# A long-convolution and recurrence block on one core: spectra and DFT tables kept as two parts in memory

## Chip, cores and metric

One Trainium2 chip, one of its cores. The metric is the time of one execution in device microseconds. The times shown are of three runs of the kernel before, and of one profiled execution of it.

## What is computed

A block over 4096 tokens of width 1024: RMSNorm, one input projection to 4608 columns, two mixers side by side, a gated norm of each, one output projection, the residual and a last norm. What matters here is the first mixer, a long convolution of 768 channels over the whole sequence, done through Fourier transforms of length 8192:

```python
def _fft_conv(u, k):
    L = u.shape[1]
    U = jnp.fft.rfft(u, n=2 * L, axis=1)
    K = jnp.fft.rfft(k, n=2 * L, axis=0)
    return jnp.fft.irfft(U * K[None], n=2 * L, axis=1)[:, :L]

        u = v * x1
        y_hy = x0 * (_fft_conv(u, kfilt) + hy_skip[l].astype(f32) * u)
```

`kfilt` comes from a small network over positions (the filter). The second mixer is a gated linear recurrence (RG-LRU) of 768 channels in both directions.

## The kernel before

Every float32 operand of a matmul is split into two parts of a type that TensorE (PE) takes in one pass, `hi` = the value rounded and `lo` = the value less `hi`; three matmuls (hi hi, hi lo, lo hi) then give the product (`mm3`, L503 to L507). A split is a ScalarE copy that rounds and a subtraction (`split`, L499 to L501).

The projection goes in steps: one step is one block of 128 of the 36 x 128 output columns for one of 8 chunks of 512 tokens, 24 matmuls (L311 to L313), 288 steps in all, in five passes over the chunks; the first pass makes the normalised input `x` in two parts and stores it (`xs`), later passes load it. The weights of a pass are loaded in halves of 256 KB (L277) and split on VectorE (L278, L279).

The transform of length 8192 is done as 128 x 64. Four stages belong to it:

- `phase_filter` (L509): a small network, and then 64 rounds, each of which makes one 128 x 768 slice of the filter, splits it into `kr`, multiplies it by the table `fa` (`first_dft`, L573 to L577), evicts the result into `kw` and stores it in `ef_d`.
- `phase_u` (L620): 32 groups of two slices of `u`; each is loaded, split into `ut` (L635, L636), multiplied by `fu`, evicted into `ustg` (L644) and stored in `eu_d` (L645).
- `phase_mid` (L653): 65 steps. Step k loads a 128 x 768 slice of `ef_d` and of `eu_d` and splits both (L658 to L660: a ScalarE copy and a GpSimd subtraction for each), loads the tables of this k (L665) and splits them on GpSimd (L669, L670), multiplies both slices by the first table, forms the complex product on VectorE (L689 to L692), splits it (`rs`, L500, L501), multiplies by the second table, evicts into `r` and stores in `ey_d` (L702, L703).
- `phase_iy` (L721): 32 groups that load two slices of `ey_d` (L736), split them into `es` (L738, L739), multiply by `fi` (L745) and store the result (L751).

`phase_lru` is the recurrence, `phase_out` (L754) the output projection; it begins when both mixers are done.

The generators are woven by `weave`: the program is written so that projection steps alternate with the steps of one other stage (filter, then recurrence, then u, mid and iy) by fixed weights. What the engines get is another order: `TileContext(..., schedule_with_timeline_sim=True)` reorders the instructions of all engines by an estimate of when each could run. The order is fixed before the run, and each engine works through its own in order; an instruction that waits holds up those behind it. All loads and stores but a few are issued by SP's queue, in one order; a load from SP waits for the eighth load or store before it to have landed.

The lines that the prediction speaks of:

## Time and profile before

| | us |
|---|---|
| median of 3 runs (lowest to highest) | 2957.67 (2956.57 to 2961.78) |
| the profiled execution, its own time | 2955.19 |
| span of the profile, first to last instruction | 2953.4 |
| PE busy | 2848.1 |
| VectorE (DVE) busy | 1997.9 |
| ScalarE (ACT) busy | 1697.9 |
| GpSimd (POOL) busy | 705.9 |

The stages by the trace: the first 8 projection steps run until about 61 us, the filter's network until about 200 us, the filter's rounds from 221 to 668 us, the recurrence from 678 to about 1400 us, u from 1402 to 1562 us, the middle stage from 1576 to 2176 us, the inverse stage from 2187 to 2343 us, the output from 2362 us on. Projection steps run beside all of them until 2329 us.

A row of a window gives the window, its length, the busy us and the number of instructions of each engine (PEld is PE's loading of weights), the share of its full clock that PE was granted, the mean busy share of the 16 DMA engines, and GB/s. "busy" of PE is not its rate: a matmul of 512 columns lasts 0.39 us, but the next starts 0.227 us after it.

### The profile page before, as it was taken

What the parts mean: (1) busy time and instruction counts of PE and PEld (TensorE: products, weight loads), DVE (VectorE), ACT (ScalarE), POOL (GpSimd) and SP (SyncE); (2) the same over time, 40 slices, a digit from 0 to 9 for tenths busy, and PEclk for the clock granted to TensorE, in tenths of its full rate; (3) what the DMA queues carried; (4) which work ended last, traced back from release to release, by engine and by line L of the source; (5) the groups of instructions that cost most, each with busy time, mean ns of one, the idle gap of its engine ahead of it and who ended that gap; (6) DMA issues with size and microseconds to landing.
All of it is one profiled execution on the core that took longest, in us unless ns stands there. A gap on an engine that the chain in (4) does not pass through costs nothing.

```text
span 2953.4 us, 37821 instructions
## 1 busy us (share of the span) xinstructions
PE 2848.1 (96%) x13211; PEld 2386.2 (81%) x13211; DVE 1997.9 (68%) x2144; ACT 1697.9 (57%) x2534; POOL 705.9 (24%) x910
## 2 busy tenths in 40 slices
PE   7999999999999999999999998999999799999998
PEld 6778888888887787877888887888888678888886
DVE  6998879664768856787664788666643366666665
ACT  4678887767787676764445675666645432222222
POOL 0013323210101201111004776766710010000001
PEclk9999999999999999999999999999999889999999
DMA  7566657437879877787997677666679865455542
GB/s 273 210 219 235 232 215 250 177 136 244 292 273 309 291 277 249 258 310 225 357 342 277 227 239 259 230 231 238 235 276 309 280 211 164 164 182 169 176 154 75
DMA packets 338238, 699.33 MB, mean 237 GB/s; under 512 B 33821, under 2 KB 156145, under 8 KB 337791
## 3 DMA queue, kind: packets, MB, share of 16 engines
q1 hardware_dynamic: 337918, 696.85, 67.9%
q8 instruction: 105, 1.72, 0.2%
q14 instruction: 87, 0.70, 0.1%
q0 software_dynamic: 128, 0.05, 0.0%
HBM read 445.13 MB, written 251.66 MB: 236 GB/s over the span
## 4 chain that ended last, share of the span: by engine, by line
PE 65%; DVE 13%; DMA 9%; issue 5%; ACT 5%; POOL 3%; SPq 1%; DVEq 0%; ACTq 0%; POOLq 0%
PE mm L311 12%; PE mm L312 12%; PE mm L313 12%; PE aux L506 8%; PE aux L819 4%; PE aux L817 4%; PE aux L818 4%; PE aux L443 3%; DVE cv L343 2%; PE aux L745 2%; DMA eu<-eud 2%; DMA x<-xs 2%; DVE sy L796 2%; PE aux L642 2%; DVE bb L470 1%
## 5 line engine op out<-in xcount | busy, mean ns | idle before, releaser
L311 PE MATMUL mm<-x,w 128*128 128x512 f32 x2304 | 909.3, 396 | 12.6 <-ACT cv L341 5.6
L312 PE MATMUL mm<-x,w 128*128 128x512 f32 x2304 | 907.6, 394 | 0.1
L313 PE MATMUL mm<-x,w 128*128 128x512 f32 x2304 | 905.2, 394 | 0.0
L311 PEld LDWEIGHTS mm<-x,w 128*128 128x128 f32 x2304 | 435.2, 189 | 105.3 <-DMA x<-xs 9.3
L313 PEld LDWEIGHTS mm<-x,w 128*128 128x128 f32 x2304 | 434.7, 189 | 84.4 <-issue 0.5
L312 PEld LDWEIGHTS mm<-x,w 128*128 128x128 f32 x2304 | 434.9, 189 | 84.1 <-issue 1.4
L817 PE MATMUL aux<-w,A 128*128 128x512 f32 x768 | 305.7, 398 | 19.0 <-DMA y<-yld 19.0
L343 DVE SCALAR_TENSOR_TENSOR cv<-raw,cols,cv 128x512 f32<-128x512 f32 (+2 forms) x336 | 260.7, 780 | 85.7 <-ACT cv L341 81.2
L819 PE MATMUL aux<-w,A 128*128 128x512 f32 x768 | 305.2, 401 | 0.0
L818 PE MATMUL aux<-w,A 128*128 128x512 f32 x768 | 304.4, 396 | 0.0
L798 POOL CAST sr<-sy 128x256 fp32r<-128x256 f32 x32 | 39.2, 1226 | 703.4 <-DVE sy L796 498.2
L660 POOL TENSOR_TENSOR ef<-ef 128x768 fp32r<-128x768 f32 x64 | 129.1, 2017 | 239.3 <-DMA eu<-eud 195.2
L817 PEld LDWEIGHTS aux<-w,A 128*128 128x128 f32 x768 | 146.1, 190 | 49.6 <-ACT A L793 19.3
L818 PEld LDWEIGHTS aux<-w,A 128*128 128x128 f32 x768 | 146.0, 190 | 32.0
L819 PEld LDWEIGHTS aux<-w,A 128*128 128x128 f32 x768 | 145.9, 190 | 30.9
L501 DVE TENSOR_TENSOR rs<-r,rs 128x768 fp32r<-128x768 f32 x65 | 94.1, 1447 | 108.3 <-ACT rs L500 108.3
L791 ACT ACTIVATE y<-y 128x1536 f32<-128x1536 f32 x32 | 47.7, 1490 | 202.8 <-DVE S L790 180.9
L333 ACT ACTIVATE raw<-mm 128x512 f32<-128x512 f32 x192 | 113.3, 590 | 86.0 <-PE mm L313 85.6
L443 PE MATMUL aux<-hl,wg 128*128 128x512 f32 x576 | 147.8, 392 | 5.4 <-ACT bb L445 5.2
L477 POOL TENSOR_TENSOR xb<-xb,bb 128x1024 f32<-128x1024 f32 x24 | 65.2, 2719 | 292.5 <-DVE bb L470 203.6
L660 POOL TENSOR_TENSOR eu<-eu 128x768 fp32r<-128x768 f32 x64 | 124.3, 1943 | 39.0 <-ACT eu L659 38.9
L443 PEld LDWEIGHTS aux<-hl,wg 128*128 128x128 f32 x576 | 107.3, 188 | 29.3 <-ACT bb L445 6.8
(201 smaller groups left out, 5023.6 us busy)
## 6 DMA issues: line engine op xcount, KB each, us to landing
x<-xs SPq DMA_DIRECT2D x256, 512.0 KB
hl<-hld SPq DMA_DIRECT2D x96, 512.0 KB
xs<-x SPq DMA_DIRECT2D x64, 512.0 KB
efd<-kw SPq DMA_DIRECT2D x64, 384.0 KB
sd<-cv SPq DMA_DIRECT2D x96, 256.0 KB
xb<-xbd SPq DMA_DIRECT2D x48, 512.0 KB
eud<-ustg SPq DMA_DIRECT2D x32, 768.0 KB
ef<-efd SPq DMA_DIRECT2D x64, 384.0 KB
```

The source lines that it names most:

```text
L311: nc.tensor.matmul(ps, lhsT=w[:, 0, kt, :], rhs=x[kt][:, 0], start=kt == 0, stop=False)
L312: nc.tensor.matmul(ps, lhsT=w[:, 0, kt, :], rhs=x[kt][:, 1], start=False, stop=False)
L313: nc.tensor.matmul(ps, lhsT=w[:, 1, kt, :], rhs=x[kt][:, 0], start=False, stop=kt == KT - 1)
L333: nc.scalar.activation(R[:, K - 1:K - 1 + TC], ps, AF.Copy)
L343: nc.vector.scalar_tensor_tensor(y[:, :N], R[:, k:k + N], w[k], y[:, :N], op0=ALU.mult, op1=ALU.add)
L443: nc.tensor.matmul(ps[:, h], lhsT=wg[:, u, gi, :], rhs=hl[h][:, v], start=k == 0, stop=k == 2)
L501: nc.vector.tensor_tensor(dst[:, 1], src, dst[:, 0].bitcast(F32), ALU.subtract)
L506: nc.tensor.matmul(ps[:, h, :NH], lhsT=lhs[:, x], rhs=rhs[:, y, h * NH:(h + 1) * NH], start=first and i == 0, stop=last and i == 2)
L660: eng.tensor_tensor(t[:, 1], raw, t[:, 0].bitcast(F32), ALU.subtract)
L817: nc.tensor.matmul(ps[:, h], lhsT=ht, rhs=w[:, 0, sl], start=b == 0, stop=False)
L818: nc.tensor.matmul(ps[:, h], lhsT=ht, rhs=w[:, 1, sl], start=False, stop=False)
L819: nc.tensor.matmul(ps[:, h], lhsT=lt, rhs=w[:, 0, sl], start=False, stop=b == CB - 1)
```

## The change

The results of the first transforms of filter and u are split when they leave PSUM: ScalarE writes the rounded part into the tile, VectorE subtracts it from PSUM into the second part, and both are stored. `ef_d` and `eu_d` have twice the size, `phase_mid` loads both parts with one load of 128 x 1536 and does no split of them. The tables are split by the host's constants into two parts (`c_tabs` has twice the size); a copy from memory to memory puts them into the scratch tensor `tab_d`, one copy of 256 KB per k, written in the filter's loop; `phase_mid` loads from there what PE uses as it is. In `phase_u` the rounding of `u` moves from VectorE to ScalarE. Rings: `kw` 3 to 2, `ustg` 3 to 2 (each of twice the size), `tab` 3 in place of `traw` 2, `tb` 2 and `ib` 2.

```diff
--- before.py
+++ after.py
@@ -104,7 +104,11 @@
     fi[64] = np.cos(math.pi * p64[0]) / 8192
     fa = fa.reshape(128, 2, 64).transpose(0, 2, 1).reshape(128, 128)
     fi = fi.reshape(2, 64, 64).transpose(1, 0, 2).reshape(128, 64)
-    return dict(c_zf=zf, c_tn=tn, c_absd=absd.astype(f), c_fa=fa.astype(f), c_tabs=np.stack([tb, ib], 2).astype(f), c_fi=fi.astype(f))
+    tabs = np.stack([tb, ib], 2).astype(f)
+    bits = tabs.view(np.uint32)
+    high = ((bits + np.uint32(0x7FF) + ((bits >> np.uint32(12)) & np.uint32(1))) & np.uint32(0xFFFFF000)).view(f)
+    tabs = np.stack([high, tabs - high], 3)
+    return dict(c_zf=zf, c_tn=tn, c_absd=absd.astype(f), c_fa=fa.astype(f), c_tabs=tabs, c_fi=fi.astype(f))
 
 
 @with_exitstack
@@ -122,8 +126,9 @@
     yl_d = [dram.tile([P, L], F32, name=f"yld{b}") for b in range(CB)]
     yf_d = [dram.tile([P, L], F32, name=f"yfd{b}") for b in range(CB)]
     s_d = [dram.tile([2, CB, P, TC], F32, name=f"sd{n}") for n in range(NCH)]
-    ef_d = dram.tile([64, 2, 64, C], F32, name="efd")
-    eu_d = dram.tile([64, 2, 64, C], F32, name="eud")
+    ef_d = dram.tile([64, 2, 64, 2, C], F32, name="efd")
+    eu_d = dram.tile([64, 2, 64, 2, C], F32, name="eud")
+    tab_d = dram.tile([P, 65, 2, 2, P], F32, name="tabd")
     ey_d = dram.tile([64, 2, 64, C], F32, name="eyd")
 
     ident = cst.tile([P, P], F32, name="ident")
@@ -569,15 +574,19 @@
             acc = fw.tile([P, C], F32, name="acc")
             nc.gpsimd.memset(acc, 0.0)
             hv3 = [t.rearrange("k (p j) -> k p j", j=64) for t in hid]
-            ev = ef_d.rearrange("k r j c -> (k r) j c")
-            def first_dft(j, kw, kr):
+            ev = ef_d.rearrange("k r j w c -> (k r) j w c")
+            def first_dft(j, kr):
                 ps = aux_ps()
                 mm3(ps, fa, kr)
-                nc.scalar.activation(cv2(kw), hv(ps), AF.Copy)
-                nc.sync.dma_start(ev[:, j, :], kw)
+                nc.scalar.activation(cv2(kr[:, 0]), hv(ps), AF.Copy)
+                nc.vector.tensor_tensor(cv2(kr[:, 1]), hv(ps), cv2(kr[:, 0].bitcast(F32)), ALU.subtract)
+                nc.sync.dma_start(ev[:, j], kr.bitcast(F32))
 
             pend = None
             for j in list(range(1, 64)) + [0]:
+                nc.sync.dma_start(tab_d[:, j], a["c_tabs"][:, j])
+                if j == 0:
+                    nc.sync.dma_start(tab_d[:, 64], a["c_tabs"][:, 64])
                 lh = lhs[j % 2]
                 for i in range(2):
                     for q in range(2):
@@ -593,7 +602,7 @@
                 mm3(ps, lr, w4)
                 if pend is not None:
                     first_dft(*pend)
-                kw = fw.tile([P, C], F32, name="kw", bufs=3)
+                kw = fw.tile([P, C], F32, name="kw", bufs=2)
                 nc.vector.tensor_tensor(cv2(kw), hv(ps), cv2(win), ALU.mult)
                 nc.scalar.activation(win, kw, AF.Abs)
                 nc.vector.tensor_tensor(acc, acc, win, ALU.add)
@@ -612,7 +621,7 @@
                     nc.vector.tensor_tensor(kw[0:1, :], kw[0:1, :], skr, ALU.add)
                 kr = fw.tile([P, 2, C], F32R, name="kr", bufs=2)
                 split(kr, kw)
-                pend = (j, kw, kr)
+                pend = (j, kr)
                 yield 0.8
             first_dft(*pend)
 
@@ -626,23 +635,24 @@
             fu = up.tile([P, 2, P], F32R, name="fu")
             nc.vector.tensor_copy(fu[:, 0], f0)
             nc.vector.tensor_tensor(fu[:, 1], f0, fu[:, 0].bitcast(F32), ALU.subtract)
-            ev = eu_d.rearrange("k r j c -> (k r) j c")
+            ev = eu_d.rearrange("k r j w c -> (k r) j w c")
             uv = ut_d.rearrange("(p j) c -> p j c", j=64)
             for g in range(64 // JB):
                 ui = up.tile([64, JB, C], F32, name="uin", bufs=3)
                 nc.sync.dma_start(ui, uv[:, g * JB:(g + 1) * JB, :])
                 t = up.tile([P, JB, C], F32R, name="ut", bufs=2)
-                nc.vector.tensor_copy(t[0:64], ui)
+                nc.scalar.activation(t[0:64], ui, AF.Copy)
                 nc.vector.tensor_tensor(t[64:], ui, t[0:64].bitcast(F32), ALU.subtract)
-                stg = up.tile([P, JB, C], F32, name="ustg", bufs=3)
+                stg = up.tile([P, JB, 2, C], F32R, name="ustg", bufs=2)
                 for j in range(JB):
                     ps = aux_ps()
                     for h in range(2):
                         for w in range(2):
                             nc.tensor.matmul(ps[:, h, :NH], lhsT=fu[:, w], rhs=t[:, j, h * NH:(h + 1) * NH],
                                              start=w == 0, stop=w == 1)
-                    nc.scalar.activation(cv2(stg[:, j]), hv(ps), AF.Copy)
-                nc.sync.dma_start(ev[:, g * JB:(g + 1) * JB, :], stg)
+                    nc.scalar.activation(cv2(stg[:, j, 0]), hv(ps), AF.Copy)
+                    nc.vector.tensor_tensor(cv2(stg[:, j, 1]), hv(ps), cv2(stg[:, j, 0].bitcast(F32)), ALU.subtract)
+                nc.sync.dma_start(ev[:, g * JB:(g + 1) * JB], stg.bitcast(F32))
                 yield WU
 
 
@@ -652,24 +662,15 @@
 
     def phase_mid():
         with tc.tile_pool(name="mid", bufs=1) as mp:
-            def load(src, s, name, eng):
+            def load(src, s, name):
                 t = mp.tile([P, 2, C], F32R, name=name, bufs=3)
-                raw = t[:, 1].bitcast(F32)
-                nc.sync.dma_start(raw, src[s].rearrange("r j c -> (r j) c"))
-                nc.scalar.activation(t[:, 0], raw, AF.Copy)
-                eng.tensor_tensor(t[:, 1], raw, t[:, 0].bitcast(F32), ALU.subtract)
+                nc.sync.dma_start(t.bitcast(F32), src[s].rearrange("r j w c -> (r j) w c"))
                 return t
 
             def tabs(k):
-                raw = mp.tile([P, 2, P], F32, name="traw", bufs=2)
-                nc.sync.dma_start(raw, a["c_tabs"][:, k])
-                r = []
-                for i, (nm, nb) in enumerate((("tb", 2), ("ib", 2))):
-                    t = mp.tile([P, 2, P], F32R, name=nm, bufs=nb)
-                    nc.gpsimd.tensor_scalar(t[:, 0], raw[:, i], 1.0, 0.0, op0=ALU.mult, op1=ALU.add)
-                    nc.gpsimd.tensor_tensor(t[:, 1], raw[:, i], t[:, 0].bitcast(F32), ALU.subtract)
-                    r.append(t)
-                return r
+                t = mp.tile([P, 2, 2, P], F32R, name="tab", bufs=3)
+                nc.sync.dma_start(t.bitcast(F32), tab_d[:, k])
+                return t[:, 0], t[:, 1]
 
             def dft(w, t):
                 ps = aux_ps()
@@ -704,7 +705,7 @@
 
             pend = None
             for k in range(64):
-                ef, eu = load(ef_d, k, "ef", nc.gpsimd), load(eu_d, k, "eu", nc.gpsimd)
+                ef, eu = load(ef_d, k, "ef"), load(eu_d, k, "eu")
                 terms = []
                 for kk in ((0, 64) if k == 0 else (k,)):
                     tb, ib = tabs(kk)
```

Line numbers after the change are a few higher (L277 becomes L282, L311 becomes L316, L506 becomes L511, L745 becomes L746; L587 is the copy of a table).

What the order makes of it, at three places.

SP's queue at the start, before (s is the staging tile of half a block of weights, `w_in`; xs the store of the normalised input):

```order
L277 DMA s_339<-in_w_in_dram 128x4x128
L277 DMA s_343<-in_w_in_dram 128x4x128
L261 DMA xs_0_60<-x 128x1024
L261 DMA xs_1_61<-x 128x1024
L277 DMA s_348<-in_w_in_dram 128x4x128
L261 DMA xs_2_62<-x 128x1024
L277 DMA s_352<-in_w_in_dram 128x4x128
L261 DMA xs_3_63<-x 128x1024
```

The same place after the change, from the same point (tabd is the scratch tensor of the tables):

```order
L587 DMA tabd<-in_c_tabs_dram 128x512 x2
L282 DMA s_340<-in_w_in_dram 128x4x128
L282 DMA s_344<-in_w_in_dram 128x4x128
L587 DMA tabd<-in_c_tabs_dram 128x512 x6
L266 DMA xs_0_60<-x 128x1024
L266 DMA xs_1_61<-x 128x1024
L282 DMA s_349<-in_w_in_dram 128x4x128
L587 DMA tabd<-in_c_tabs_dram 128x512 x2
```

Eight copies stand ahead of the third half block and, with two behind the rows shown, twelve ahead of the fourth; before, none.

SP's queue a little later, after the change (the half blocks are the second half of the fourth block of weights and the two of the fifth; xbd and hld are stores of the recurrence's input; there is no copy at this place before):

```order
L282 DMA s_371<-in_w_in_dram 128x4x128
L587 DMA tabd<-in_c_tabs_dram 128x512 x10
L353 DMA xbd_125<-cv 128x510
L587 DMA tabd<-in_c_tabs_dram 128x512 x13
L282 DMA s_376<-in_w_in_dram 128x4x128
L587 DMA tabd<-in_c_tabs_dram 128x512 x5
L393 DMA hld_138<-cv 128x510
L587 DMA tabd<-in_c_tabs_dram 128x512
L391 DMA hld_139<-cs 128x510
L587 DMA tabd<-in_c_tabs_dram 128x512 x4
L282 DMA s_380<-in_w_in_dram 128x4x128
```

Thirty-three of the 65 copies stand between these three loads; six more come before the second half of the sixth block of eight, and none after it.

PE's order at the last projection step, before (mm is the projection, es and fi are of the inverse stage, A is the output stage):

```order
L312 MATMUL mm<-x,w 128x512
L313 MATMUL mm<-x,w 128x512
L311 MATMUL mm<-x,w 128x512
L312 MATMUL mm<-x,w 128x512
L313 MATMUL mm<-x,w 128x512
L745 MATMUL aux<-es,fi 128x384 x60
L817 MATMUL aux<-w,A 128x512
L818 MATMUL aux<-w,A 128x512
L817 MATMUL aux<-w,A 128x512
L818 MATMUL aux<-w,A 128x512
```

The last five groups of the inverse stage, 60 matmuls, are all that stands between the projection and the output stage. After the change (ef, eu and rs are of the middle stage; tab is the table):

```order
L511 MATMUL aux<-rs,tab 128x384 x5
L316 MATMUL mm<-x,w 128x512
L317 MATMUL mm<-x,w 128x512
L318 MATMUL mm<-x,w 128x512
L511 MATMUL aux<-ef,tab 128x384 x6
L511 MATMUL aux<-eu,tab 128x384 x6
L511 MATMUL aux<-rs,tab 128x384 x6
L511 MATMUL aux<-ef,tab 128x384 x6
```

and the end of the same stretch:

```order
L511 MATMUL aux<-rs,tab 128x384 x6
L511 MATMUL aux<-ef,tab 128x384 x6
L511 MATMUL aux<-eu,tab 128x384 x6
L511 MATMUL aux<-rs,tab 128x384 x17
L746 MATMUL aux<-es,fi 128x384 x384
L818 MATMUL aux<-w,A 128x512
L819 MATMUL aux<-w,A 128x512
L818 MATMUL aux<-w,A 128x512
```

Between the last projection matmul and the first of the output stage now stand 22 of the 65 steps of the middle stage (132 matmuls of ef, 132 of eu, 138 of rs) and all 384 matmuls of the inverse stage. Counted the same way, the filter's rounds now lie among 69 projection steps (51 before), the recurrence's matmuls among 82 (90), those of u among 41 (20), and the middle stage begins after 238 of the 288 steps (208).

## Rows read from the trace of the kernel before

**Rows 1.** The page, part 1: span, and busy us and share of each engine.

```profile
span 2953.4 us, 37821 instructions
...
PE 2848.1 (96%) x13211; PEld 2386.2 (81%) x13211; DVE 1997.9 (68%) x2144; ACT 1697.9 (57%) x2534; POOL 705.9 (24%) x910
```

**Rows 2.** Stages: window; busy us (count) PE, PEld, DVE, ACT, POOL; PEclk; DMA; GB/s.

```profile
0.00:55.00 55.00, 42.35 (x183) 33.50 (x184) 37.24 (x80) 24.68 (x60) 3.06 (x11) 1.00 0.92 322
...
200.00:668.00 468.00, 467.48 (x2316) 407.94 (x2316) 352.32 (x478) 359.83 (x630) 140.62 (x389) 1.00 0.57 209
...
1400.00:1576.00 176.00, 173.13 (x802) 149.85 (x803) 100.69 (x84) 71.80 (x118) 0.00 (x0) 0.98 0.97 341
1576.00:2176.00 600.00, 574.63 (x2714) 490.65 (x2713) 418.23 (x376) 400.36 (x546) 404.66 (x388) 1.00 0.69 238
...
2330.00:2380.00 50.00, 26.59 (x113) 21.57 (x112) 21.48 (x16) 16.85 (x16) 6.53 (x4) 0.76 0.88 304
```

**Rows 3.** Waits of PE in the middle stage, and the longest of all.

```profile
PE aux L817 <- DMA y<-yld: 19.0, 1, 19.0
PE aux L506 <- DVE rs L501: 11.0, 15, 1.5
```

**Rows 4.** Instruction groups by line, middle stage.

```profile
L660 POOL TENSOR_TENSOR ef<-ef 128x768 fp32r<-128x768 f32 x64 | 129.1, 2017 | 239.3 <-DMA eu<-eud 195.2 <-ACT ef L659 44.1
...
L689 DVE TENSOR_TENSOR us<-aux,hb 64x768 f32<-64x768 f32 x65 | 62.4, 959 | 54.0 <-ACT hb L685 53.2
...
L659 ACT ACTIVATE ef<-ef 128x768 fp32r<-128x768 f32 x64 | 54.1, 845 | 35.3 <-DMA ef<-efd 32.4 <-POOL tb L670 2.6
```

**Rows 5.** The tile r and its split: durations in ns, min/median/max.

```profile
L692 DVE SCALAR_TENSOR_TENSOR r<-us,sgn,r x65: 1014/1216/2616, 1595.0 to 2168.3; 128x768 f32<-128x768 f32 x65
...
L501 DVE TENSOR_TENSOR rs<-r,rs x65: 946/1175/2619, 1597.1 to 2170.2; 128x768 fp32r<-128x768 f32 x65
```

**Rows 6.** Order of time, VectorE: start us, us, instruction, wait before it.

```profile
54.52 0.43 DVE L278 CAST w<-s 128x512 fp32r<-128x512 f32 x1 [0.33 <-DMA s<-in_w_in_dram]
```

**Rows 7.** Window with the highest DMA rate (columns as in rows 2).

```profile
2260.00:2270.00 10.00, 10.00 (x52) 9.05 (x51) 3.52 (x2) 4.75 (x5) 0.00 (x0) 1.00 1.02 412
```

**Rows 8.** Order of time, PE: two matmuls that stand 24 matmuls apart.

```profile
40.34 0.39 PE L311 MATMUL mm<-x,w 128*128 128x512 f32 x1
...
45.78 0.39 PE L311 MATMUL mm<-x,w 128*128 128x512 f32 x1
```

**Rows 9.** Chain of waits: start us, us, what; 23 matmuls of the inverse stage.

```profile
2322.12 4.01 PE aux L745 x23
```

**Rows 10.** Order of time, PE: the last groups of the inverse stage.

```profile
2335.07 2.35 PE L745 MATMUL aux<-es,fi 128*128 128x384 f32 x12 [1.35 <-DVE es L739]
...
2337.81 2.36 PE L745 MATMUL aux<-es,fi 128*128 128x384 f32 x12 [0.39 <-DVE es L739]
...
2341.32 2.19 PE L745 MATMUL aux<-es,fi 128*128 128x384 f32 x11 [1.15 <-DVE es L739]
```

**Rows 11.** Chain of waits at the end of the inverse stage and beyond.

```profile
2337.99 1.49 ACT es L738
2339.51 1.77 DVE es L739
...
2343.59 0.82 ACT yo L749
2344.43 0.45 SPq L751
2344.92 2.67 DMA ytd<-yo
...
2348.25 4.52 DMA o<-in_x_dram
```

**Rows 12.** Windows after PE had stopped (columns as in rows 2).

```profile
2350.00:2360.00 10.00, 0.00 (x0) 0.00 (x0) 1.76 (x1) 0.40 (x1) 0.00 (x0) 0.50 1.04 374
2360.00:2370.00 10.00, 6.17 (x14) 4.48 (x15) 8.88 (x6) 6.36 (x6) 3.93 (x2) 0.50 1.05 376
```

## Prediction

> **What bounds the kernel now.** I read the busy shares first: the reader is to see TensorE (PE) busy for 2848.1 of 2953.4 us [rows 1], so only 105 us of its idle time could be won, and whatever newly makes it wait is added to the end. Then the busy time by stage [rows 2]: PE idles 25.4 us in the stage of the products of the spectra (1576 to 2176 us, "the middle stage" below), 12.7 us in the first 55 us and 23.4 us from 2330 to 2380 us, and hardly at all while the filter is made (0.5 us in 468). The same rows show the DMA: 0.92 busy in the first 55 us, 0.97 in the stage of u's spectra, 0.69 in the middle stage. A full DMA moves 341 / 0.97 = 352 GB/s [rows 2]. Last the waits of PE: in the middle stage its largest is 11.0 us for the split of the product [rows 3]; the largest of all, 19.0 us, is for the first loads of the output stage, which the change leaves alone. So at most some 25 us can be won where the change takes work away, and the room for what it adds is the DMA's.
>
> **Work removed.** In each of 64 steps of the middle stage two ScalarE copies of 0.845 us and two GpSimd subtractions of some 2.0 us go [rows 4], and the four GpSimd instructions of each table. VectorE's two instructions without PSUM there take 1.216 and 1.175 us at the median and 1.014 and 0.946 at their shortest [rows 5]; with GpSimd quiet I expect the shortest. None of it is PE's own work; it can win back at most the 25.4 us. I take 10, because the loads that replace it fill the DMA (below): bounds 25 won and 15 lost.
>
> **Copies of the tables at the start.** The 65 copies depend on nothing, and the order puts all of them among the first loads on SP: 12 ahead of the second half of the second tile of weights, 26 ahead of the second half of the fourth, all 65 ahead of the last five halves. Each moves 128 x 512 x 4 bytes, 17.04 MB in all. No row shows a copy from memory to memory. If the DMA engines do it at 352 GB/s it takes 48 us; the first 55 us leave 8% of the DMA idle, 4.4 us, so the last weights come 44 us later. Now they are cast at 54.52 us, right after their arrival [rows 6], and PE's eighth step, which uses them, is then under way, so that I count 1 us to spare. So **+43 us**, on the path, since PE has nothing else in its order. Lower bound: 17.04 MB at the best 10 us on record, 412 GB/s [rows 7], less 4.4 and 1, gives +36. Upper bound: if a byte read and a byte written in memory each take a transfer's place, 34.1 MB need 97 us, +92. I take the first because GB/s over share stays between 345 and 367 in all stages of [rows 2], whatever their mix of loads and stores. The Trainium skill, "DMA: Bandwidth & Descriptors", section "Where 436 GB/s comes from", says that between HBM and SBUF the memory side, some 358 GB/s per core, is what binds; by that a copy inside the memory would pay twice and the sum would be 49 us higher. The trace speaks half against it: 412 GB/s [rows 7] lies above that figure.
>
> **Filter and u.** In the filter stage the first part is evicted as before, into kr, and VectorE gains 64 subtractions from PSUM at 0.959 us (that of another PSUM operand in [rows 4]), 61 us; it is busy 352 of 468 us there [rows 2], and the order now spreads the stage over 69 projection steps instead of 51, so they fit. The store doubles and a kr tile is free only when it has landed, in a ring of two: +3 us, bounds 0 and 30. In the stage of u a cast moves from VectorE to ScalarE, which is busy 72 of 176 us; hidden. The stores double: 32 groups now move 1.97 MB each, and the 41 projection steps that the order now lays among them (20 before) some 0.86 MB each (eight 512 KB tiles per seven steps and a 256 KB store): 98 MB, 278 us at 352 GB/s. PE's own work there is 41 steps x 24 matmuls, 5.44 us a step by [rows 8], and 256 matmuls at 4.01 / 23 = 0.174 us [rows 9]: 268 us. **+10 us**, bounds 0 and 30.
>
> **The middle stage beside projections.** A step now loads 2 x 768 KB and a 256 KB table and stores 384 KB, 2.23 MB. 43 of 65 steps stand beside the last 50 projection steps: 96 + 43 = 139 MB, 395 us of DMA, against PE work of 50 x 5.44 + 43 x 18 x 0.174 = 407 us. The DMA is at 97%; that is why I took 10 of 25 above.
>
> **The tail, the largest term.** The order shows what the text of the change doesn't: because filter and u are stretched, the projections run out sooner. Before, only 60 matmuls of the inverse stage stood behind the last projection; now 22 steps of the middle stage (402 matmuls) and all 384 of the inverse stage do, with nothing beside them. Alone, a middle step takes the longest of PE 3.14 us, VectorE 3 x 0.96 + 1.01 + 0.95 = 4.84 us and DMA 2.23 MB / 352 = 6.3 us. 22 x 6.3 = 139 us less PE's 70: **+69 us**. Bounds: 36 at VectorE's pace, 84 at 7 us a step (the DMA at 0.9 of its rate). A group of the inverse stage alone moves 1.18 MB, 3.35 us; its last groups before, alone too, started 2.74 and 3.51 us apart [rows 10]. 32 x 3.35 = 107 less PE's 67, less the 3 us that were idle before: **+37**, bounds 18 (2.74 us) and 42. Between the two stages every product must land before the inverse loads; that was covered by projections and now stands bare: eviction 0.82, issue 0.45, store 2.67, load 4.52, copy 1.49, subtraction 1.77 us, by the nearest links of the chain [rows 11], **+12**, bounds 5 and 15.
>
> **Sum.** 43 + 3 + 10 - 10 + 69 + 12 + 37 = +164 us on the profiled execution's 2955.2 us, 3119; the runs' median, 2957.7, is 2.5 us above it, so **3120 us** rounded.
>
> **Rivals.**
> Dear copies: copies inside the memory pay for reading and for writing. For it: the trace has none, and the DMA is full there anyway. It gives +92 for +43: 3169 us. Chance 0.18.
> Half clock in the tail: once PE had stopped at 2343.5 us [rows 10], its granted clock was 0.50 in the windows from 2350 us on, also while work ran again [rows 12]; half of full is 1.2 of 2.4 GHz. PE is half idle throughout the new tail. At twice 0.174 us, PE needs 6.3 us for a middle step, as long as its loads, and 4.2 instead of 3.35 for an inverse group: +27 us, 3147. Against it: in the middle stage PE idles in small pieces, 25 us of 600, at a clock of 1.00 [rows 2]. Chance 0.12. The Trainium skill, "TensorE: Matmul & The Clock Gate", section "Part 1: The HAM clock gate (the "warmup" mystery)", says that the chip's default is the low clock and only activity lifts it; the trace agrees at 2350 us [rows 12], and by that rule this rival would be the likelier the emptier the tail is.
> Light tail: DMA and chains overlap better than I sum, the tail goes at VectorE's pace and 2.74 us a group: 69 becomes 36 and 37 becomes 18, 3068 us. Chance 0.15.
> Faster: the relief of VectorE and ScalarE in the middle stage decides. If the loads hide as they do at a share of 0.69, all 25.4 us come back and nothing else shows: 2932 us. It needs a middle step without projections to take no more than PE's 3.14 us; five VectorE instructions of 0.95 to 1.01 us speak against that, whatever the DMA does. Chance 0.03.
> Gains and costs could also cancel: 0.01.
>
> **Numbers.** The forecast itself has 0.51. About 0.2% (6 us) is what a measurement of this kernel can tell from no change. Slower: 0.51 + 0.18 + 0.12 + 0.15 = 0.96; faster 0.03; the same 0.01. All low bounds together give 2957.7 + 36 + 0 + 0 - 25 + 36 + 5 + 18 = 3028, all high ones 2957.7 + 92 + 30 + 30 + 15 + 84 + 15 + 42 = 3266; that all fall on one side is unlikely, so the range is 3035 to 3215: below it the light tail still fits, above it only dear copies with a dear tail are left out.
>
> **What would show it.** Right, if the profile of the changed kernel has: PE idle some 55 us in the first 105 us, waiting for weights (through VectorE's casts); the first 100 us at a DMA share near 1; GpSimd idle in the middle stage; VectorE's product instructions near 1.0 us; after the last projection a stretch of about 255 us in which PE is half busy, DMA near 1 in its first part; the output stage as long as before. Wrong, if the last of the first eight weights is cast before 70 us, if PE is over 80% busy in the tail, or if the filter stage shows PE waiting for kr by more than 30 us.

## The result and the profile after

The changed kernel takes 3141.39 us (median of 4 runs, 3133.83 to 3144.46); the kernel before, run beside it, 2957.12 us. The ratio is 1.063, with a 95% interval from 1.0615 to 1.0646. The profiled execution took 3133.83 us. The forecast was 3120 us in a range from 3035 to 3215.

The page of the changed kernel, part 1 (span; busy us and share of each engine; answers to [rows 1]):

```profile
span 3132.1 us, 37272 instructions
...
PE 2902.4 (93%) x13211; PEld 2426.7 (77%) x13211; DVE 2005.1 (64%) x2240; ACT 1660.6 (53%) x2443; POOL 285.5 (9%) x522
```

The span is 178.7 us longer. PE is idle for 229.7 us instead of 105.3, and for the same 13211 matmuls it is busy 54.3 us longer, in part because some of them ran at a slower clock, as shown below. GpSimd has lost 420 us of work, and the time is longer all the same.

Windows of the changed kernel by stage, columns as in [rows 2], which they answer: the start in two parts, the filter's rounds, the recurrence, u, the middle stage beside projections, its steps behind the last projection, the gap to the inverse stage, the inverse stage, the wait for the output's first loads.

```profile
0.00:55.00 55.00, 29.52 (x102) 20.75 (x103) 21.88 (x50) 16.86 (x41) 3.02 (x11) 0.91 0.94 347
55.00:105.00 50.00, 30.38 (x101) 22.53 (x100) 20.78 (x36) 11.68 (x30) 0.00 (x0) 0.76 1.01 333
278.00:813.00 535.00, 530.76 (x2587) 458.15 (x2585) 407.82 (x538) 361.81 (x634) 121.14 (x353) 1.00 0.64 240
813.00:1448.00 635.00, 603.88 (x2669) 495.29 (x2670) 462.37 (x480) 465.22 (x617) 72.30 (x53) 0.98 0.84 288
1495.00:1750.00 255.00, 247.54 (x1125) 209.14 (x1124) 126.61 (x120) 118.42 (x169) 0.00 (x0) 0.99 0.96 343
1800.00:2231.00 431.00, 430.99 (x2058) 376.65 (x2057) 215.18 (x227) 207.88 (x276) 0.00 (x0) 1.00 0.91 334
2232.00:2397.00 165.00, 109.10 (x403) 95.02 (x401) 105.80 (x112) 90.43 (x114) 0.00 (x0) 0.77 0.78 272
2397.00:2406.00 9.00, 0.00 (x0) 0.00 (x0) 0.99 (x3) 1.96 (x2) 0.00 (x0) 0.50 0.62 201
2406.00:2524.00 118.00, 87.53 (x384) 75.89 (x384) 56.28 (x32) 69.16 (x63) 0.00 (x0) 0.89 0.89 303
2524.00:2543.00 19.00, 0.20 (x2) 0.00 (x0) 3.45 (x4) 3.67 (x3) 0.00 (x0) 0.56 0.88 288
```

Read three things here. The DMA is full in the first 105 us, while PE starts 203 matmuls where it had started 183 in the first 55 us alone. Beside projections the middle stage has no idle time left (430.99 of 431 us). And behind the last projection PE works through 402 matmuls of the middle stage in 165 us and through 384 of the inverse stage in 118, with a clock of 0.77 and 0.89.

VectorE of the changed kernel in order of time, three of the casts of the first weights, columns as in [rows 6]:

```profile
51.29 0.43 DVE L283 CAST w<-s 128x512 fp32r<-128x512 f32 x1 [8.64 <-DMA s<-in_w_in_dram]
...
78.96 0.43 DVE L283 CAST w<-s 128x512 fp32r<-128x512 f32 x1 [9.56 <-DMA s<-in_w_in_dram]
...
104.21 0.42 DVE L283 CAST w<-s 128x512 fp32r<-128x512 f32 x1
```

The last of the first eight weights is cast at 104.21 us instead of 54.52 [rows 6], and the casts wait for the loads. The 65 copies were issued from 12 to 88 us.

PE's waits in the changed kernel from 2232 to 2406 us (us in all, times, longest), the stretch in which the middle stage stands alone:

```profile
PE aux L511 <- DMA tab<-tabd: 20.3, 11, 3.9
PE aux L511 <- ACT rs L505: 20.2, 12, 2.5
PE aux L511 <- DVE rs L506: 12.5, 7, 2.5
```

The chain of waits of the changed kernel there (start us, us, what):

```profile
2252.03 5.54 PE aux L511 x18
2257.59 6.32 DMA tab<-tabd
2264.05 4.58 PE aux L511 x17
2268.64 6.59 DMA tab<-tabd
2275.37 5.79 PE aux L511 x18
2281.18 5.18 DMA tab<-tabd
```

So the chain goes from a table's load to a step's 18 matmuls and, through the table tile that they free, to the next load. One turn of it, about 11.2 us, covers one and a half steps (nine turns and 239 matmuls from 2242 to 2343 us), so it gives 7.6 us a step. Both links are longer than I had counted. A load lands 5 to 6.6 us after its issue, and 18 matmuls take about 5.2 us instead of 18 x 0.174 = 3.1 [rows 9]. The second is in the main the clock, as two groups of instructions of the changed kernel show (by line; busy us, mean ns), first from 2232 to 2397 us, then from 1850 to 2231 us:

```profile
L511 PE MATMUL aux<-ef,tab 128*128 128x384 f32 x132 | 38.4, 441 | 22.4 <-DMA tab<-tabd 20.3 <-ACT r L703 1.0 <-issue 0.8
...
L511 PE MATMUL aux<-ef,tab 128*128 128x384 f32 x240 | 48.8, 338 | 0.0
```

Two windows of 10 us in that stretch of the changed kernel (columns as in [rows 2]) show the same: PE busy two thirds and half, its clock at 0.67 and 0.83, a mixture of 1.2 and 2.4 GHz.

```profile
2310.00:2320.00 10.00, 6.62 (x21) 5.46 (x20) 6.26 (x8) 5.52 (x7) 0.00 (x0) 0.67 0.90 290
...
2330.00:2340.00 10.00, 5.47 (x20) 4.67 (x20) 7.44 (x9) 4.67 (x6) 0.00 (x0) 0.83 0.95 351
```

VectorE's instructions without PSUM became short, as hoped; the tile r of the changed kernel (durations in ns), columns as in [rows 5], where the medians were 1216 and 1175:

```profile
L693 DVE SCALAR_TENSOR_TENSOR r<-us,sgn,r x65: 1010/1019/1021, 1828.7 to 2391.8; 128x768 f32<-128x768 f32 x65
...
L506 DVE TENSOR_TENSOR rs<-r,rs x65: 948/959/960, 1832.0 to 2393.8; 128x768 fp32r<-128x768 f32 x65
```

### The profile page after: what moved, and what is told of

Read it like the earlier page. It is cut to its first block, busy times and chain, and to the rows that moved or that the text cites. A ratio compares the mean times of both kernels' runs of the same rounds, so it can differ in the third digit from the quotient of the medians.

```text
span 3132.1 us, 37272 instructions
## 1 busy us (share of the span) xinstructions
PE 2902.4 (93%) x13211; PEld 2426.7 (77%) x13211; DVE 2005.1 (64%) x2240; ACT 1660.6 (53%) x2443; POOL 285.5 (9%) x522
## 4 chain that ended last, share of the span: by engine, by line
PE 70%; DMA 10%; DVE 9%; ACT 5%; issue 4%; POOL 1%; SPq 1%; DVEq 0%; ACTq 0%; POOLq 0%
PE mm L316 14%; PE mm L318 13%; PE mm L317 13%; PE aux L511 10%; PE aux L820 4%; PE aux L818 4%; PE aux L819 4%; PE aux L448 3%; DMA tab<-tabd 2%; DMA s<-in_w_in_dram 2%; PE aux L651 1%; DVE sy L797 1%; DVE bb L475 1%; DMA e<-eyd 1%; DVE cv L348 1%
## 5 line engine op out<-in xcount | busy, mean ns | idle before, releaser
L316 PE MATMUL mm<-x,w 128*128 128x512 f32 x2304 | 915.2, 399 | 60.7 <-DVE w L283 30.5
L316 PEld LDWEIGHTS mm<-x,w 128*128 128x128 f32 x2304 | 437.6, 190 | 161.1 <-ACT cv L346 19.8
L690 DVE TENSOR_TENSOR us<-aux,hb 64x768 f32<-64x768 f32 x65 | 62.3, 959 | 201.6 <-ACT hb L686 171.2
L409 ACT ACTIVATE cv<-mm 128x512 f32<-128x512 f32 x96 | 57.2, 597 | 137.3 <-PE mm L318 125.1
L511 PE MATMUL aux<-rs,tab 128*128 128x384 f32 x390 | 95.3, 364 | 32.9 <-ACT rs L505 20.2
L746 PE MATMUL aux<-es,fi 128*128 128x384 f32 x384 | 87.7, 381 | 39.7 <-DVE es L740 24.7
```

The costliest lines, as they stand in the source:

```text
L316: nc.tensor.matmul(ps, lhsT=w[:, 0, kt, :], rhs=x[kt][:, 0], start=kt == 0, stop=False)
L511: nc.tensor.matmul(ps[:, h, :NH], lhsT=lhs[:, x], rhs=rhs[:, y, h * NH:(h + 1) * NH], start=first and i == 0, stop=last and i == 2)
L690: nc.vector.tensor_tensor(cv2(us)[0:64], pu[64:], cv2(hb)[64:], ALU.mult)
L746: nc.tensor.matmul(ps[:, h, :NH], lhsT=fi[:, fp, i], rhs=es[:, ep, i, h * NH:(h + 1) * NH], start=m == 0, stop=m == 5)
```

## Experiments

Each is compared with the kernel before on the same chip, whose median there was 2952.9 to 2957.1 us. "Alone" is what stands behind the last projection: middle steps and inverse groups by PE's order, and the time from the start of the last projection matmul to the end of the last inverse matmul by the trace.

| kernel | us | ratio (95%) | alone: steps, groups | us alone |
|---|---|---|---|---|
| before | 2957.1 | 1 | 0, 5 | 15.0 |
| the change | 3141.4 | 1.0630 (1.0615 to 1.0646) | 22, 32 | 292.5 |
| copies_alone | 3003.2 | 1.0158 (1.0136 to 1.0179) | 0, 5 | 15.0 |
| copies_in_filter | 3114.4 | 1.0534 (1.0507 to 1.0561) | 22, 32 | 297.8 |
| filter_part_alone | 2947.8 | 0.9978 (0.9964 to 0.9991) | 0, 14 | 47.6 |
| u_part_alone | 2992.6 | 1.0116 (1.0094 to 1.0138) | 2, 32 | 154.6 |
| tables_alone | 2952.6 | 0.9993 (0.9982 to 1.0005) | 0, 14 | 48.9 |
| filter_and_u | 3046.4 | 1.0303 (1.0280 to 1.0326) | 16, 32 | 238.1 |
| u_ring_of_three | 3100.8 | 1.0492 (1.0467 to 1.0516) | 12, 32 | 219.2 |
| table_ring_of_four | 3109.7 | 1.0518 (1.0499 to 1.0537) | 19, 32 | 258.8 |
| half_loads | 3108.2 | 1.0522 (1.0504 to 1.0540) | 16, 32 | 247.3 |
| whole_change_other_rings | 3037.6 | 1.0286 (1.0270 to 1.0303) | 0, 21 | 77.2 |
| filter_and_tables | 2935.1 | 0.9940 (0.9925 to 0.9955) | 0, 3 | 8.6 |
| tables_ring_of_four | 2925.2 | 0.9907 (0.9892 to 0.9923) | 0, 3 | 9.6 |

**The start.** copies_alone adds to the kernel before (whose host then keeps each table twice, so that the copies have their size; the middle stage loads one of the two)

```diff
             for j in list(range(1, 64)) + [0]:
+                nc.sync.dma_start(tab_d[:, j], a["c_tabs"][:, j])
+                if j == 0:
+                    nc.sync.dma_start(tab_d[:, 64], a["c_tabs"][:, 64])
```

> The kernel before, plus the 65 copies of 256 KB from memory to memory and nothing else of the change; nothing reads what they write, and PE's order is that of the kernel before. Theory (the copies push the first weights back, and PE has nothing else to do): the last weight of the first eight is cast near 104 us instead of 54.5, as in the changed kernel, and the time is 2957 + 48 = 3005 us, give or take 6. Rival 1 (the delay at the start is taken up by slack later, and the whole excess of the changed kernel comes from its end): under 2970 us. Rival 2 (what was late at the start was also late through the other parts of the change, a later order of the loads): between 2970 and 2995.

Measured 3003.16 us, +48.1. VectorE in order of time, the last cast of the first eight weights:

```profile
104.85 0.42 DVE L281 CAST w<-s 128x512 fp32r<-128x512 f32 x1
```

The delay at the start (50.3 us by this cast) reaches the end almost in full; rivals 1 and 2 fall. copies_in_filter is the changed kernel with

```diff
-                nc.sync.dma_start(tab_d[:, j], a["c_tabs"][:, j])
+                tbn = fw.tile([P, 2, 2, P], F32, name="tbn")
+                nc.sync.dma_start(tbn, a["c_tabs"][:, j])
+                nc.sync.dma_start(tab_d[:, j], tbn)
```

(and the same for table 64).

> The changed kernel, with each table copied through an SBUF tile of the filter stage (one buffer, a load and a store) instead of directly, so that the copies run beside the filter's rounds and not at the start. PE's order is that of the changed kernel. Theory: the first eight weights are cast by 55 us again, the filter's rounds have DMA to spare, and the time is 3141 - 48 = 3093 us, give or take 8. Rival (the copies cost their DMA time wherever they stand, since something waits for DMA there too): 3125 us or more, with PE idle in the filter stage.

Measured 3114.35: 27 us won, not 48, between the theory and the rival. The start is as before (last cast at 54.13 us), but the filter gives back a part. During its rounds ScalarE's split of the next slice waits for the store that must free its tile, 46.5 us from 200 to 750 us (27.5 us from 278 to 813 in the changed kernel), and where the filter's last rounds stand without projections PE is idle for 26 of 50 us; at the same place the changed kernel loses 13 (800 to 830 us). The stretch alone is 5 us longer, too. That is 18 of the 21 us. ScalarE's wait in copies_in_filter, from 200 to 750 us (us in all, times, longest):

```profile
ACT kr L505 <- DMA efd<-kr: 46.5, 32, 3.2
```

The window of copies_in_filter at the end of the rounds (columns as in [rows 2]):

```profile
750.00:800.00 50.00, 23.58 (x85) 17.75 (x84) 18.68 (x27) 15.38 (x20) 2.86 (x6) 0.64 0.59 219
```

**The parts one by one.** filter_part_alone, u_part_alone and tables_alone each make one part of the change in the kernel before. In tables_alone the copies are left out, and GpSimd's queue loads the host's two parts straight into the ring:

```diff
-                nc.sync.dma_start(t.bitcast(F32), tab_d[:, k])
+                nc.gpsimd.dma_start(t, a["c_tabs"][:, k])
```

> The kernel before with the filter's part of the change alone: the filter's spectrum is split when it leaves PSUM and stored as two parts, u and the tables stay as they were. PE's order: filter among 69 projection steps, 168 matmuls of the inverse stage (14 groups) behind the last projection, no middle steps there. Theory (what costs is the work that the order leaves behind the last projection): 9 more inverse groups than before stand alone, each 3.7 us instead of 2.1 of PE, +14; filter +3; relief in the middle stage -6; 2968 us, between 2955 and 2985. Rival (the cost of the two splits is their DMA volume, about half of the 135 us that the changed kernel loses outside its start): 3015 to 3030 us.

Measured 2947.77 us: 7 us faster than before, below the range that I gave. The rival by volume is out by 67 us or more. I had counted 6 us of relief; it is 24, since the middle stage has no idle time left (1576 to 2176 us of filter_part_alone, 574.63 busy before [rows 2]):

```profile
1576.00:2176.00 600.00, 599.13 (x2884) 525.72 (x2883) 384.20 (x386) 365.95 (x502) 265.13 (x324) 1.00 0.84 304
```

> The kernel before with u's part of the change alone. PE's order: u among 40 projection steps instead of 20, and behind the last projection 3 middle steps and all 32 inverse groups. Theory (work left behind the last projection): inverse groups alone 27 x (3.7 - 2.1) = +43 over the five of before, boundary between middle and inverse stage +12, three middle steps +11, u itself 0 to +10, relief of the middle stage -6 to -10: 3005 to 3030 us, 3020 the likeliest. Rival (DMA volume): the same saving and cost as the filter's part alone, within 10 us of that kernel.

Measured 2992.58, +37.5, below my range for the same reason: PE idles 2 us in the middle stage (1710 to 2233 us). It is 45 us above the filter's part, which has the same traffic (both read and write 25 MB more than before), so that volume is not what makes the difference.

> The kernel before with the tables' part alone, and without its copies: the host's two parts are loaded straight into the ring of three table tiles, issued by GpSimd, which has nothing else to do there; filter and u as before. PE's order: filter, recurrence and u as before, 14 inverse groups behind the last projection. Theory (order): like the filter's part alone, which has the same 14 groups there, 2940 to 2960 us, with the waits for POOL gone. Rival (the ring of three, whose tile is freed only by the inverse matmuls of its step, stops PE in the middle stage too and carries the 105 us that filter and u do not explain): 3000 us or more, with PE waiting for tab by over 40 us.

Measured 2952.56, the same as before within the interval. PE waits 6.7 us for tab in the middle stage; the rival falls.

**The parts together.** The three parts alone sum to -7 + 37 - 3 = +27, and the copies make it 75; the change costs 184. filter_and_u asks where the other 109 come from.

> The kernel before with the filter's and u's parts of the change; the tables are loaded and split on GpSimd as before, so there are no copies. PE's order: 16 middle steps and all 32 inverse groups behind the last projection (the filter's part alone leaves none and 14, u's alone 2 and 32). Theory (what costs is what stands behind the last projection, so the parts do not add): 2955 - 7 (filter alone) + 37 (u alone) + 14 further middle steps alone at 7.0 us instead of the 3.2 of PE's own work, +53: 3038 us, between 3020 and 3055. Rival (each part has its own price, wherever the order puts it): 2955 - 7 + 37 = 2985 us, give or take 8; then the tables' part would carry the other 105 us of the change.

Measured 3046.44, 91 us over before where the two prices add to 30. The parts do not add: one stretches the filter, the other u, and only together do they use up the projections with 16 steps of the middle stage still to do. With the copies this makes 139 of the 184 us. Of the other 45 some 42 lie in the middle steps alone, where the change has 22 of 7.4 us and filter_and_u 16 of 6.4 (below), each above PE's 3.14. u_ring_of_three takes some of that back without touching the traffic:

```diff
-                stg = up.tile([P, JB, 2, C], F32R, name="ustg", bufs=2)
+                stg = up.tile([P, JB, 2, C], F32R, name="ustg", bufs=3)
```

> The changed kernel with three instead of two staging tiles for u's spectra. PE's order: u among 30 projection steps instead of 41, the middle stage from step 224 instead of 238, and 12 middle steps behind the last projection instead of 22. Theory (order): 10 steps fewer alone, 10 x (7.0 - 3.2) = -38 us, 3103, between 3090 and 3115. Rival (memory traffic sets the time from u on, so that what leaves the end is waited for in the stage of u): 3130 to 3145 us, with PE idle between 1500 and 1750 us by 25 us or more (4 us in the changed kernel).

Measured 3100.81, -40 us against the change. PE is idle 10 us from 1500 to 1750 us, not the 25 of the rival.

**What bounds a step of the middle stage alone.** Two edits of the changed kernel: table_ring_of_four has a fourth table tile; half_loads leaves the second parts of ef and eu in memory.

```diff
-                t = mp.tile([P, 2, 2, P], F32R, name="tab", bufs=3)
+                t = mp.tile([P, 2, 2, P], F32R, name="tab", bufs=4)
```

```diff
-                t = mp.tile([P, 2, C], F32R, name=name, bufs=3)
-                nc.sync.dma_start(t.bitcast(F32), src[s].rearrange("r j w c -> (r j) w c"))
-                return t
+                t = mp.tile([P, 1, C], F32R, name=name, bufs=3)
+                nc.sync.dma_start(t[:, 0].bitcast(F32), src[s][:, :, 0].rearrange("r j c -> (r j) c"))
+                return t.broadcast_to([P, 2, C])
```

> The changed kernel with four instead of three table tiles; PE's order has 19 middle steps behind the last projection instead of 22. Theory (in the tail each table comes late because its tile is freed only one step before it is needed): the steps alone go from 7.0 to the 6.3 us of their transfers and PE's wait for tab, 20.3 us in all, falls below 8: -13 for that and -11 for three steps less, 3117 us. Rival (the transfers themselves are the bound, the wait only shows up under the table's name since it is issued last): the steps stay at 7.0 us, only the three steps count, 3130 us, and the wait moves to ef or eu.

> The changed kernel without the loads of the second parts of both spectra (768 KB a step instead of 1536, 1.44 MB with table and store instead of 2.23); the matmuls that used the second parts use the first ones again, so that PE does as much as before. Stores, copies and rings as in the changed kernel; PE's order has 16 middle steps behind the last projection instead of 22. Theory 1 (transfers bound a step of the tail): 1.44 MB at 352 GB/s are 4.1 us, VectorE's 4.84 us become the bound, a step goes from 7.4 to about 5 us, and the time is 3141 - 6 x 4.2 - 16 x 2.4 = 3077 us, give or take 10. Theory 2 (the ring of three tables bounds it: a table is asked for when the inverse matmuls of three steps back are done, and lands 5 to 6.6 us later): a step stays above 6.3 us, PE waits for tab as before, 3105 us, give or take 10.

A step is the time of the stretch by its matmuls over 18. In the changed kernel it is 164.8 / (402 / 18) = 7.4 us; with the ring of four 133.4 / (354 / 18) = 6.8; with half the loads 116.3 / (293 / 18) = 7.1; and in filter_and_u, where GpSimd splits the tables into rings of two, 104.3 / (294 / 18) = 6.4. PE's longest waits in the stretch, table_ring_of_four (2235 to 2369 us):

```profile
PE aux L511 <- ACT rs L505: 15.4, 14, 2.0
PE aux L511 <- DVE rs L506: 10.6, 11, 2.5
PE aux L511 <- ACT hb L686: 6.2, 5, 2.5
```

and half_loads (2256 to 2373 us):

```profile
PE aux L511 <- DMA tab<-tabd: 12.4, 7, 4.0
PE aux L511 <- ACT rs L505: 12.1, 8, 2.5
```

The chain of waits of half_loads, two of its table loads (start us, us, what):

```profile
2290.85 4.25 DMA tab<-tabd
...
2335.47 3.47 DMA tab<-tabd
```

The windows of table_ring_of_four, half_loads and filter_and_u there (columns as in [rows 2]):

```profile
2235.00:2369.00 134.00, 90.96 (x356) 75.04 (x354) 97.46 (x101) 79.91 (x100) 0.00 (x0) 0.85 0.81 293
...
2256.00:2372.00 116.00, 80.75 (x293) 70.63 (x291) 75.69 (x81) 65.27 (x82) 0.00 (x0) 0.75 0.58 182
...
2206.00:2310.00 104.00, 72.78 (x296) 61.38 (x294) 77.44 (x82) 65.90 (x82) 28.15 (x59) 0.84 0.78 289
```

With the DMA at 0.58 a table lands 3.2 to 4.3 us after its issue instead of 5 to 6.6, but a step is hardly shorter and the wait for tab stays; so transfers alone do not bound the step. With one tile more that wait is gone, and the step is 6.8 us, not 6.3: PE then waits for the product and its split, at a clock of 0.85, and the DMA at 0.81 has room. The times, 3108.18 (theory 2: 3105) and 3109.72 (theory: 3117), say less than the steps: a step that no longer stands alone saves 4.2 us (7.4 less PE's 3.14), so 25 of half_loads's 33 us and 13 of table_ring_of_four's 32 come from the order.

So the ring of three is the chain that ends last in the changed kernel, and close behind it come the product's chain and the clock. By the windows PE is busy for 4.9 us a step in the changed kernel, 4.6 with four tiles, 5.0 with half the loads and 4.5 in filter_and_u, where I had reckoned with 3.14, and idle for 2.5, 2.2, 2.2 and 1.9 us. Four tiles and half the loads together, and what the clock alone costs, were not tried.

**The whole change with its work covered.** whole_change_other_rings takes the direct loads of tables_alone with four tiles, ustg 3, and

```diff
-NX = 12
+NX = 8
```

> The whole change without its copies (the host's two parts are loaded straight into the table ring by GpSimd), with four table tiles, three staging tiles in u, and 8 instead of 12 tiles of x, so that projection steps cannot run so far ahead. PE's order: no middle step and 21 inverse groups behind the last projection (22 and 32 in the changed kernel). Same memory traffic as the changed kernel but for the 17 MB of copies. Theory (order and copies are the whole cost): the filter's part alone has 14 groups there and takes 2948 us; 7 more at 3.7 - 2.0 = +12, and 5 for u: 2965 us, between 2945 and 2985. Rival 1 (doubled traffic of the spectra costs by itself): 3040 us or more. Rival 2 (8 tiles of x are too few: PE waits for x at each of 40 changes of the chunk): 3000 us or more, with waits for x over 40 us.

Measured 3037.62: 104 us better than the change, but 73 above my figure, and close to rival 1's bound. PE's waits over the whole of whole_change_other_rings:

```profile
PE mm L316 <- ACT cv L346: 25.7, 19, 5.9
PE mm L316 <- DMA x<-xs: 22.3, 24, 3.0
PE aux L743 <- DVE es L737: 22.0, 19, 1.4
```

The first two were 5.6 and 5.1 us in the kernel before. The wait for x, rival 2's sign, grew by 17 us and stays under its 40; that the 20 us more for ScalarE (cv) also come from the smaller ring of x is not shown. The 77 us alone, less before's 15 and PE's work for 16 groups (33), are 29. That is 66 of the 85 us that this kernel takes longer than the one before. How much of it all is the doubled traffic (the DMA share is 1.01 from 1450 to 1700 us, where PE idles 17 us) stays open, so that it is not shown that the traffic of both parts together has no price of its own.

**Versions that beat the kernel before.** tables_ring_of_four is tables_alone with four table tiles (the edit of table_ring_of_four); filter_and_tables is that with the filter's part and

```diff
-NX = 12
+NX = 10
...
-                kr = fw.tile([P, 2, C], F32R, name="kr", bufs=2)
+                kr = fw.tile([P, 2, C], F32R, name="kr", bufs=3)
```

> The kernel before with the filter's part and the tables' part, tables loaded straight by GpSimd into a ring of four, kr ring 3 instead of 2, x ring 10 instead of 12 (for the room); u as before. PE's order: 3 inverse groups behind the last projection, 5 in the kernel before. Theory: the middle stage's idle time goes (25 us before, 1 us with the filter's part alone) and nothing comes behind the last projection: 2955 - 25 + 10 for the change from filter to recurrence = 2940 us, between 2930 and 2948. Rival (the x ring or GpSimd's issuing gives it back): 2948 to 2965.

> The kernel before with the tables' part alone, loaded straight by GpSimd, into a ring of four instead of the three of the run with the tables alone (2952.6 us, with 14 inverse groups behind the last projection and PE waiting 6.7 us for tab in the middle stage). PE's order: 3 inverse groups behind the last projection. Theory: 11 groups more are covered, 11 x 1.0, and the wait for tab goes: 2940 us, between 2932 and 2948. Rival (the groups behind the last projection cost little when PE was not idle before them, since the filter's part alone has 14 and is faster than before): 2948 to 2954.

Measured 2935.07 and 2925.22 us, the second 0.9% faster than before and better than I expected. The middle stage and the inverse stage of tables_ring_of_four, then those of tables_alone (columns as in [rows 2]):

```profile
1560.00:2140.00 580.00, 575.34 (x2750) 503.55 (x2749) 413.37 (x378) 404.08 (x553) 283.59 (x193) 0.99 0.78 269
...
2151.00:2314.00 163.00, 161.18 (x789) 143.29 (x788) 61.33 (x41) 82.91 (x91) 0.00 (x0) 0.99 0.87 296
...
1588.00:2195.00 607.00, 590.88 (x2814) 514.73 (x2813) 407.62 (x373) 401.94 (x543) 276.91 (x188) 0.99 0.74 255
...
2207.00:2346.00 139.00, 125.72 (x615) 110.89 (x613) 61.49 (x41) 78.41 (x82) 0.00 (x0) 0.99 0.89 303
```

PE idles 4.7 us in the first, 25.4 before [rows 2]. One table tile more, 2 KB in each partition, turned a part that was worth nothing into one of 28 us. Of that PE's idle time shows 23: 16 us become 5 in the middle stage, and 13 become 2 in the inverse stage, where the ring of three had left 14 groups behind the last projection and the ring of four leaves 3.

## Why the prediction was right

The sign, the mechanism and the size held: 3141 against 3120, because the loss was where the order of instructions said, at the start and behind the last projection. That the sum came so near is partly luck, as the terms show:

- **Start, +43 expected.** 49.7 us by the last cast, 48.1 by copies_alone, more than the sum by about the 5.4 us that I had taken off as room. Dear copies (+92) are excluded: 17.04 MB in 48.1 us are 354 GB/s, the rate at which a full DMA moves loads and stores [rows 2]. The section "Where 436 GB/s comes from" of the Trainium skill's page "DMA: Bandwidth & Descriptors" gives some 358 GB/s per core as the limit on the memory side; that a copy inside the memory would pay twice against it was my inference, and the measurement decides against it.
- **Filter, +3; u, +10.** PE waited 3.5 us for kr. Not counted was the change from filter to recurrence, where projections had been drawn forward: PE idles 31 us from 813 to 1448 us, 20 us before from 700 to 1400. In u PE idles 7.5 us in 255, 2.9 in 176 before [rows 2], +5.
- **Middle stage beside projections, -10.** It was -25, all that could be won. I had held 15 back because the DMA would be full; at a share of 0.91 it still hid all its loads.
- **Middle steps alone, +69; this step failed in its reason and its size.** I wrote that a step takes the longest of PE, VectorE and DMA, and took 6.3 us of transfers, with a DMA share near 1. It took 7.4: 164.8 us less PE's 70 are +95, above my upper bound of 84. The DMA was at 0.78 and moved 272 GB/s. What I left out was that a table tile is freed only by the inverse matmuls of its step, so that its next load and PE's work stand in a chain and not beside each other; that the product and its split are a second such chain, for which PE waits most once the ring has four tiles (6.8 us a step); and that PE, partly at half clock, is busy for 4.9 us of a step and not 3.14.
- **Inverse stage alone, +37; boundary, +12.** 118 - 67 - 3 = +48 and 9 us: 3.7 us a group instead of 3.35, at a clock of 0.89 and a DMA share of 0.89.
- **Rivals.** The half clock in the tail, given 0.12, came true in part: 441 ns a matmul against 338. I had set it up as a case beside the forecast; it was a part of it. The light tail (VectorE's pace) never came near, since VectorE was busy 106 of 165 us.

The tail cost 34 us more than reckoned and the middle stage 15 less, so the sum was closer than its terms, by luck. The measured terms add to 193 us, 14 more than the spans differ by; that remainder I have not traced.

## What to carry to other kernels

Work that covers a stage is a stock: count, in the order that the engines really get, how much of it is left behind its last instruction, since two edits that each cost little (-7 and +37 us here) can together use it up (+91). Where a stage then runs alone, look for its chains before reckoning with bandwidth, first of all for the ring whose tile is freed latest: a step of 7.4 us became 6.8 with one table tile more, and still took 7.1 with half its loads. A ring's size also changes the order: one table tile more was worth 28 us in tables_ring_of_four. And a copy without a dependency was issued first here, however late it stands in the program; 17 MB of them in front of the first weights cost 48 us.

## What was not expected of the hardware

A copy from memory to memory cost no more than a load of its size does at a full DMA (352 GB/s [rows 2]): copies_alone reads and writes 17.04 MB more than the kernel before, and ran 48.1 us longer. PE's clock fell although PE was never idle for more than some 4 us at a time: busy 109 of 165 us, it was granted 0.77, while at 96% busy in the middle stage before [rows 2] it kept 1.00; the page "TensorE: Matmul & The Clock Gate" of the Trainium skill, section "Part 1: The HAM clock gate (the "warmup" mystery)", says that activity releases the throttle, and these rows agree. Over 10 us it need not go that way: of the two windows shown above, the busier (6.62 us) had the lower clock, 0.67, and the other (5.47 us) 0.83.
